# Block maxima over TensorE instead of a DRAM trip, a new load order in the setup, and a second key buffer

## The chip, the cores and the metric

The kernel runs on one core of one Trainium2 chip. The metric is the device time of one execution in microseconds (us); the figure that counts is the median of several executions.

## The reference, cut to what matters

One decoding step of a hybrid block for a prompt of 2048 tokens and 64 sample tokens (NT = 2112 columns) that share the weights:

```python
ada = silu(c) @ w_ada + b_ada            # shift, scale, gate
h = rmsnorm(x) * (1 + scale) + shift
proj = h @ w_in                          # 1024 x 11272, all projections at once
o_att = dilated attention of 8 heads over 3 groups, dilation 1, 4, 16, window 128,
        group outputs weighed by their softmax denominators
a = (o_att * silu(z_a)) @ w_pa
m = mLSTM branch, chunkwise recurrence @ w_pm
y = x + gate * ((sigmoid(g_a) * a + sigmoid(g_m) * m) @ w_out)
```

All of it is float32, and the kernel reaches that accuracy with fp16 matmuls: each 1024 x 128 block of weights is divided by a power of two near its largest magnitude and split into a high and a low fp16 half, and a product is three matmuls (high by high, low by high, high by low).

## The kernel before, in words

The program runs in stages. The **setup** loads `w_ada` in eight pieces (`wa_load`, L439; `ada_cols`, L474), normalises x, builds the halves `hh` and `hl` of h, and splits the first Q, K and V blocks (`first`). The **attention** takes 12 units in a row, 4 head pairs by 3 groups (`units`). While unit i computes scores, softmax and values (`attn`), the projections of unit i+1 (`fill`), the statistics, mixing and weighing of the pair just finished (`late`, L1334) and the splitting of the weights of the unit after that (`prepare`, L1045) are woven in. Then come the mLSTM **recurrence**, the **gates** stage (`all_gates`, L2237, the gate projections in tiles j = 1 to 7, woven with the attention of the sample tokens, `all_samples`, which reads the caches in `kt` and `vt` tiles; after them the steps `f_step` that load, measure and split the last weights), and the **output** stage.

What sets the order: `weave` (L615) runs several generators by their stated costs, and TensorE executes in just that order (its instructions are stamped). VectorE (DVE), ScalarE (ACT), GpSimd (POOL) and SyncE (SP, which issues most loads) execute each in the order the scheduler gave them; `behind()` (L226) keeps an operation behind the last one traced on DVE and ACT.

The way of a weight block, in class `Blocks`: `measure_pieces` reduces each block along its rows on DVE (L257) into a column of `mx`; then the maximum over the 128 partitions is needed in all partitions. Before the change there are two ways for it. One is a trip through DRAM on POOL's queue: `max_begin` writes the columns to `md` (L209) and reads them back broadcast to all partitions into `mb` (L212), and `max_end` reduces that on DVE (L217). The other, used in the setup and for the last weights, is TensorE: `pow2_begin` transposes the columns, padded to 128 x 128 (`zpad`, L183), DVE reduces the rows (L186), and `pow2_end` broadcasts the result with a small matmul (L191) that DVE reads (L193). Either way DVE then makes the scale `wsc`, ACT writes the high half (L281), DVE the low half (L282), and from the same maximum DVE makes `iqk` (L919 to L923), which the scores of the next unit need.

```python
 def max_begin(mx, n, mb=None):
     md = dr.tile([4, P], F32, tag="md", bufs=4, name="md")
     nc.gpsimd.dma_start(dview(md, 0, [[1, P], [P, n]]), mx)
...
     nc.gpsimd.dma_start(mb[:, :n], dview(md, 0, [[0, P], [P, n], [1, P]]))
```

Other names: `pr` is a tile of scores (DVE L1096, then ACT's exponential L1099, then its transpose on TensorE L1107 into `pTs`, then the values L1121); `ktok` (one buffer) holds keys turned to tokens, which SP writes out; `wb` the group weights that `weigh` (L1245) multiplies onto `og`; `whl` the split halves, `wr` a raw block; `ps_mm`, `ps_t`, `ps_s`, `ps_o` are PSUM banks.

Of the kernel before, what the change touches and what calls it, by code (L numbers as in the profile page):

```python
# [19 lines left out]
P = 128  # L20
# [17 lines left out]
ZM = 16  # L38
# [66 lines left out]
def trunk(ctx: ExitStack, tc: tile.TileContext, I, C, O, dbg=None, stop=None):  # L105
# [25 lines left out]
    def pst():  # L131
        return bank("t")
# [34 lines left out]
    zrow = [const.tile([P, 1], F32, name=f"zrow{k}") for k in range(4)]  # L167
    for t in zrow:
        nc.gpsimd.memset(t, 0.0)

    def max_room(pool):
        zpad[:] = [pool.tile([P, P], F32, name=f"zpad{k}") for k in range(1)]
        for t in zpad:
            nc.gpsimd.memset(t, 0.0)

    def max_cols():

        zpad.append(zpad.pop(0))
        return zpad[-1]

    def pow2_begin(mx, n):
        pt = pst()
        nc.tensor.transpose(pt[:, :P], mx, ident)  # L183
        zrow.append(zrow.pop(0))
        m1 = zrow[-1]
# [17 lines left out]
    def max_all(mx, n, mb=None):  # L203

        return max_end(max_begin(mx, n, mb), n)

    def max_begin(mx, n, mb=None):
        md = dr.tile([4, P], F32, tag="md", bufs=4, name="md")
        nc.gpsimd.dma_start(dview(md, 0, [[1, P], [P, n]]), mx)  # L209
        if mb is None:  # L210
            mb = small.tile([P, 2, P], F32, tag="mb", bufs=2, name="mb")
# [24 lines left out]
    class Blocks:  # L236
# [16 lines left out]
        def measure_pieces(self, way=None):  # L253
            n = self.n
            mx = max_cols() if way else small.tile([P, n], F32, tag="mx", name="mx")
            for i, (r, nk, nw) in enumerate(self.raws):
                nc.vector.tensor_reduce(mx[:, i:i + 1], r[:, :nk, :nw], axis=AX.XY, op=OP.max, apply_absolute_value=True)  # L257
                if i + 1 < n:
                    yield
            if way:  # L260
                self.p2, self.mb = way(mx, n), None
            else:
                self.mb = max_begin(mx, n, cur["mb"]() if n > 2 else None)
# [28 lines left out]
        def measure(self, way=None):  # L292
            for _ in self.measure_pieces(way):
                pass
# [71 lines left out]
    with sbuf("setup", side="right") as su:  # L366
# [78 lines left out]
        max_room(su)  # L445
# [9 lines left out]
        first = Blocks([w_in[:, o:o + P] for o in (QO, KO, VO)], inv_sh, WFLOOR)  # L455
# [24 lines left out]

        rows = su.tile([56, P], F32, name="rows")
        nc.sync.dma_start(rows[0:32], I["conv_w"][0].rearrange("j (a p) -> (j a) p", p=P))
        for k, nm_ in enumerate(("conv_b", "m_norm", "m_skip")):
            nc.sync.dma_start(rows[32 + 8 * k:40 + 8 * k], I[nm_][0].rearrange("(a p) -> a p", p=P))
        pt = pss()
        nc.tensor.transpose(pt[:, :56], rows, ident[:56, :56])
        chp = su.tile([P, 56], F32, name="chp")
        nc.vector.tensor_copy(chp, pt[:, :56])
        sc = su.tile([96, 2, P], F32, name="sc")
        nc.sync.dma_start(sc, I["state_conv"][0].rearrange("b j (k p) -> (b j k) p", p=P).rearrange("(a r) p -> r a p", a=2))  # L490
        pt = pss()
        for a in range(2):
            nc.tensor.transpose(pt[:, a * 96:(a + 1) * 96], sc[:, a], ident[:96, :96])
        scT = su.tile([P, 8, 24], F32, name="scT")
        nc.vector.tensor_copy(scT, pt[:, :192].rearrange("p (r k) -> p k r", k=8))

        rt = su.tile([32, 24], F32, name="rt")
        nc.sync.dma_start(rt, I["rel_table"])
        oh = su.tile([32, 3, BANDL], F32, tag="oh", name="oh")
        nc.sync.dma_start(oh, C["onehot"])  # L500
# [1937 lines left out]
```

## Time and profile before

| what | value |
|---|---|
| median of 3 executions | 3099.41 us (3095.2 to 3103.61) |
| the profiled execution, its own time | 3101.56 us |
| its span | 3099.8 us |
| TensorE (PE) busy | 2919.9 us, 94% |
| DVE, ACT, POOL busy | 1534.0, 895.7, 355.2 us |
| mean granted TensorE clock | 0.978 of full |
| DMA, mean over the span | 116 GB/s |

Busy time tells which engine carries the kernel; where it stands idle, and for whom, is in the waits. In a row of the timeline the first number is the start in us, the second the duration, and the bracket at the end holds the time that the engine stood idle just before, and who ended it. PEclk is the clock that TensorE was granted, 1.00 for 2.4 GHz and 0.50 for 1.2 GHz. An engine that is off the path may wait for nothing.

### The profile page before, as it was taken

How to read it: one execution, taken by the hardware profiler on the slowest of the kernel's cores; microseconds unless marked ns; L12 is line 12 of the kernel's file. 1: busy time of each engine (PE TensorE's matmuls, PEld its weight loads, DVE VectorE, ACT ScalarE, POOL GpSimd, SP SyncE). 2: the span in 40 equal slices, each digit the busy share in tenths (PEclk: the TensorE clock that was granted, in tenths of full speed). 3: DMA queues.
4: the chain of work that ended last, by engine and by line, in shares of the span. 5: the costliest groups of instructions: out<-in, count | busy, mean ns of one | idle time of the engine just before them, and what ended most of it. 6: DMA issues, size and time to landing. Idle time of an engine off the chain costs nothing. (4 is left out here: it accounts for less than half of the span.)

```text
span 3099.8 us, 49229 instructions
## 1 busy us (share of the span) xinstructions
PE 2919.9 (94%) x19725; PEld 1573.5 (51%) x19725; DVE 1534.0 (49%) x3832; ACT 895.7 (29%) x2002; POOL 355.2 (11%) x500
## 2 busy tenths in 40 slices
PE   6799999999999999999999999999799989999998
PEld 3455554555555545545455555555465544544443
DVE  4544445444544354475676766755322235445443
ACT  3333332333243224422232222322222223222211
POOL 0100021001101010111111111100100011011011
PEclk9899999999999999999999999999899999999999
DMA  9023332232223232153556433213777753433321
GB/s 326 19 87 96 110 85 69 88 111 83 72 88 108 87 107 55 34 141 102 157 126 204 103 96 92 64 44 76 232 235 222 212 151 123 135 124 115 103 89 61
DMA packets 272825, 358.87 MB, mean 116 GB/s; under 512 B 35348, under 2 KB 204324, under 8 KB 270548
## 3 DMA queue, kind: packets, MB, share of 16 engines
q1 hardware_dynamic: 258500, 242.89, 27.2%
q0 software_dynamic: 14096, 112.83, 11.6%
q8 instruction: 155, 2.54, 0.4%
q14 instruction: 74, 0.61, 0.1%
HBM read 292.99 MB, written 150.04 MB: 143 GB/s over the span
## 5 line engine op out<-in xcount | busy, mean ns | idle before, releaser
L587 PE MATMUL ps_mm<-hh,whl 128*128 128x512 f16 (+1 forms) x3072 | 1022.6, 350 | 17.8 <-ACT whl L281 4.8
L588 PE MATMUL ps_mm<-hl,whl 128*128 128x512 f16 (+1 forms) x3072 | 1022.9, 349 | 0.0
L589 PE MATMUL ps_mm<-hh,whl 128*128 128x512 f16 (+1 forms) x3072 | 1018.4, 349 | 2.2 <-DVE whl L282 2.2
L589 PEld LDWEIGHTS <-whl 128*128 128x128 f16 x3104 | 301.3, 99 | 311.7 <-issue 12.1
L587 PEld LDWEIGHTS <-whl 128*128 128x128 f16 x3104 | 303.9, 99 | 267.1 <-issue 48.8
L588 PEld LDWEIGHTS <-whl 128*128 128x128 f16 x3104 | 301.2, 99 | 243.7 <-issue 21.3
L1099 ACT ACTIVATE pr<-pr,nm 128x256 f32<-128x256 f32 (+1 forms) x384 | 172.7, 450 | 248.0 <-DVE nm L1096 247.6
L1096 DVE CUSTOM_DVE_ANT_0 pr<-ps_s,bias,iqk 128x256 f32<-128x256 f32 (+1 forms) x384 | 141.2, 420 | 92.9 <-PE ps_s L1090 92.9
L1107 PE MATMUL ps_t<-ident,pr 128*128 128x128 f32 x600 | 105.7, 282 | 36.2 <-ACT pr L1099 25.1
L281 ACT ACTIVATE whl<-wr,wsc 128x1024 f16<-128x1024 f32 x80 | 89.0, 1140 | 128.4 <-DVE wsc L200 116.2
L1107 PEld LDWEIGHTS ps_t<-ident,pr 128*128 128x128 f32 x600 | 76.5, 143 | 82.2 <-ACT pr L1099 44.0
L282 DVE SCALAR_TENSOR_TENSOR whl<-wr,wsc,whl 128x1024 f16<-128x1024 f32 x80 | 100.6, 1281 | 35.3 <-ACT whl L281 34.9
L2379 DVE SCALAR_TENSOR_TENSOR tgl<-tgl,ps_mm 128x512 f32<-128x512 f32 x64 | 44.0, 687 | 131.0 <-PE ps_mm L589 131.0
L157 DVE COPY pTs<-ps_t 128x512 f32<-128x512 f32 (+1 forms) x93 | 52.2, 562 | 114.0 <-PE ps_t L1107 113.9
L589 PE MATMUL ps_o<-wouh,gtl 128*128 128x512 f16 (+1 forms) x272 | 103.1, 379 | 0.2 <-DVE gtl L2401 0.2
L587 PE MATMUL ps_o<-wouh,gth 128*128 128x512 f16 (+1 forms) x272 | 103.1, 379 | 0.2 <-DVE y L2346 0.2
L588 PE MATMUL ps_o<-woul,gth 128*128 128x512 f16 (+1 forms) x272 | 103.1, 379 | 0.0
L1121 PE MATMUL ps_o<-pTs,v 128*64 128x128 f32 x1200 | 89.6, 284 | 10.1 <-DVE pTs L157 9.7
L152 ACT ACTIVATE pTs<-ps_t 128x512 f32<-128x512 f32 (+1 forms) x99 | 50.3, 508 | 164.3 <-PE ps_t L1107 164.3
L588 PE MATMUL ps_mm<-mlo,wpmh 128*128 128x512 f16 x256 | 97.0, 379 | 0.0
L587 PE MATMUL ps_mm<-mhi,wpmh 128*128 128x512 f16 x256 | 97.0, 379 | 0.0
L589 PE MATMUL ps_mm<-mhi,wpml 128*128 128x512 f16 x256 | 97.0, 379 | 0.0
(538 smaller groups left out, 4146.2 us busy)
## 6 DMA issues: line engine op xcount, KB each, us to landing
out_dram<-in_cache_kv_w_dram POOLq DMA_DIRECT2D x32, 2040.0 KB, 9.6
wr<-in_w_in_dram SPq DMA_DIRECT2D x80, 512.0 KB
kt<-in_cache_kv_w_dram SPq DMA_DIRECT2D x104, 256.0 KB
vt<-in_cache_kv_w_dram SPq DMA_DIRECT2D x104, 256.0 KB
tgl<-tg_d SPq DMA_DIRECT2D x64, 256.0 KB
out_dram<-in_cache_kv_w_dram POOLq DMA_DIRECT2D x8, 2016.0 KB, 14.8
tg_d<-tg POOLq DMA_DIRECT2D x56, 256.0 KB, 3.9
xt<-in_x_prompt_dram SPq DMA_DIRECT2D x24, 512.0 KB
```

The source lines that it names most:

```text
L152: nc.scalar.activation(out, in_, AF.Copy)
L157: nc.vector.tensor_copy(out, in_)
L281: nc.scalar.activation(hv, rv, AF.Copy, scale=s[:, i:i + 1])
L282: nc.vector.scalar_tensor_tensor(lv, rv, s[:, i:i + 1], hv, op0=OP.mult, op1=OP.subtract)
L587: nc.tensor.matmul(out, lhsT=ah, rhs=bh, start=first, stop=False)
L588: nc.tensor.matmul(out, lhsT=ah, rhs=bl, start=False, stop=False)
L589: nc.tensor.matmul(out, lhsT=al, rhs=bh, start=False, stop=last)
L1096: nc.vector.tensor_tensor_reduce(pr[ti][:, h, :nk], pS[h][:, a:b], bias[:, h, W - nk:W], scale=iqk[:, 2:3], scalar=3.0e38, op0=OP.add, op1 ...
L1099: nc.scalar.activation(pr[ti][:, h, :nk], pr[ti][:, h, :nk], AF.Exp, scale=-1.0, bias=nm[:, h, ti:ti + 1], accum_out=sm[:, h, ti:ti + 1])
L1107: nc.tensor.transpose(pT[:, (h * nb + b2) * P:(h * nb + b2 + 1) * P], pr[ti][:, h, b2 * P:(b2 + 1) * P], ident)
L1121: nc.tensor.matmul(po[h * 64:h * 64 + 64, jc:jc + P], lhsT=x["v"][(k0 + b2) // 4][:, (k0 + b2) % 4, h * 64:h * 64 + 64], rhs=pTs[ti][:, h ...
L2379: nc.vector.scalar_tensor_tensor(tg[:, :n], tg[:, :n], 1.0, pb[:, :n], op0=OP.add, op1=OP.mult)
```

## The change

- The TensorE way becomes the rule in `Blocks`; only the recurrence keeps the DRAM trip (`measure(True)`). Its first half is a step of its own, `turn()` (transpose and row reduce), and its second half (the broadcast) stands at the split. 21 of 32 trips are replaced: 42 DMAs fewer on POOL's queue, 21 transposes and 21 broadcast matmuls more on PE. `turn()` is placed a step ahead of the split in `prepare`, `last_mix`, `z_last` and `all_gates`.
- `zpad` becomes four pads, in a pool that stays; the broadcast of the last weights goes to another PSUM bank (`room=pss`).
- The setup loads all eight `wa` pieces right behind the first quarter of x, then the first weight blocks; the small tables (`rows`, `sc`, `rel_table`, `onehot`, `band`) and what is computed of them move behind the loads of the other quarters of x. The first split stands behind all of `ada_cols`.
- `ktok` gets a second buffer.
- `late` mixes first, then does the next unit's projections and turns, and weighs last, each step of it with 1.25 times its cost.
- In the gates stage the measuring of block pair 2 moves from the end of the recurrence to the gate tile j = 1, the splits of pairs 2 and 3 move back by some steps, and the next load as well.

```diff
-    def pow2_end(m1, n, floor=2.0 ** -100):
-        pb = pst()
+    def pow2_end(m1, n, floor=2.0 ** -100, room=pst):
+        pb = room()
...
-        def measure_pieces(self, way=None):
+        def measure_pieces(self, dram=False):
             n = self.n
-            mx = max_cols() if way else small.tile([P, n], F32, tag="mx", name="mx")
+            self.mx = small.tile([P, n], F32, tag="mx", name="mx") if dram else max_cols()
...
+        def turn(self):
+            self.m1 = pow2_begin(self.mx, self.n)
...
-            p2 = self.p2 if self.mb is None else max_end(self.mb, n)
-            to_pow2(p2, self.floor)
+            if self.mb is not None:
+                p2 = max_end(self.mb, n)
+                to_pow2(p2, self.floor)
+            else:
+                if self.m1 is None:
+                    self.turn()
+                p2 = pow2_end(self.m1, n, self.floor)
...
         for q in range(NWA):
             ada_cols(q)
-
-        rows = su.tile([56, P], F32, name="rows")
...
+            wa_load(NWA + q)
+        first = Blocks([w_in[:, o:o + P] for o in (QO, KO, VO)], inv_sh, WFLOOR)
         with behind():
             x_norm(x0)
-        first.measure(pow2_of)
+        for q in range(NWA, 8):
+            ada_cols(q)
+        first.measure()
         first.split(later=True)
-        for q in range(NWA, 8):
-            wa_load(q)
-            ada_cols(q)
...
-                kt = at.tile([P, 4, P], F32, tag="ktok", bufs=1, name="ktok")
+                kt = at.tile([P, 4, P], F32, tag="ktok", bufs=2, name="ktok")
...
             if step:
+                with behind():
+                    ahead.turn()
+                yield
                 yield from queued(ahead.split_pieces())
...
             if units[i][1] == 2:
-                yield from combine(i)
+                begin_combine(i)
+                yield from tail[3]()
             yield 1
...
+            if units[i][1] == 2:
+                for cost in tail[4]():
+                    yield 1.25 * cost
...
-    def f_split(i):
...
-        p2 = pow2_end(m1, 1)
+        p2 = pow2_end(m1, 1, room=pss)
...
                     if j == 1 and at == 0:
                         with behind():
+                            pend[2].measure()
+                    if j == 1 and at == 1:
+                        with behind():
+                            pend[2].turn()
+                    if j == 1 and at == 3:
+                        with behind():
                             pend[2].split()
                             pend[3].measure()
+                    if j < 6 and at == GS[0] - 2 + 5 * (j == 1):
+                        with behind():
+                            pend[j + 2].turn()
...
-                    if j < 6 and at == GS[0]:
+                    if j < 6 and at == GS[0] + 4 * (j == 1):
                         with behind():
                             pend[j + 2].split()
```

How the rows of the engines move, at three places. First DVE, in the attention, at the split of the four blocks of unit 5 (at 555 us in the trace of before); before:

```order
L159 TENSOR_SCALAR vT<-ps_mm,wun 128x4x128
L257 TENSOR_REDUCE mx<-wr 128x1
L157 COPY pTs<-ps_t 128x512
L217 TENSOR_REDUCE p_5224<-mb_5197 128x4
L221 TENSOR_SCALAR p_5224<-p_5224 128x4
L222 TENSOR_SCALAR p_5224<-p_5224 128x4
L199 RECIPROCAL wsc<-p_5224 128x4
L267 TENSOR_SCALAR wun<-p_5224,inv_sh 128x4
L200 TENSOR_SCALAR wsc<-wsc 128x4
L919 TENSOR_SCALAR iqk<-wun,qk_e 128x2
```

After the change, the same place up to the row reduce:

```order
L269 TENSOR_REDUCE zpad<-wr 128x1
L1293 TENSOR_REDUCE amax<-zall 128x1
L159 TENSOR_SCALAR vT<-ps_mm,wun 128x4x128
L269 TENSOR_REDUCE zpad<-wr 128x1
L157 COPY pTs<-ps_t 128x512
L198 TENSOR_REDUCE zrow_70<-ps_t 4x1
L1123 ISA pr,nm<-ps_s,bias,iqk 128x256
```

and, after four pairs of score rows (L1123, was L1096), the split itself:

```order
L157 COPY og<-ps_o 128x16x32
L954 SCALAR_TENSOR_TENSOR QS<-ps_mm,qk_e,QS 128x4x128
L208 TENSOR_SCALAR p_5302<-ps_t 128x4
L209 TENSOR_SCALAR p_5302<-p_5302 128x4
L214 RECIPROCAL wsc<-p_5302 128x4
L281 TENSOR_SCALAR wun<-p_5302,inv_sh 128x4
L215 TENSOR_SCALAR wsc<-wsc 128x4
L937 TENSOR_SCALAR iqk<-wun,qk_e 128x2
L944 TENSOR_SCALAR uq<-wun 128x1
```

The reduce of the DRAM trip's tile (L217) is gone. In its place the short row reduce (L198) follows the last block's maximum, scores come between, and the scale begins with L208, which reads the broadcast of TensorE.

Second SP, the loads of the setup; before:

```order
L441 DMA wa<-in_w_ada_dram 128x8x256 x4
L412 DMA xt<-in_x_prompt_dram 128x1024 x4
L250 DMA wr<-in_w_in_dram 128x8x128 x3
L482 DMA rows<-in_conv_w_dram 32x128
L484 DMA rows<-in_conv_b_dram 8x128
L484 DMA rows<-in_m_norm_dram 8x128
L484 DMA rows<-in_m_skip_dram 8x128
L490 DMA sc<-in_state_conv_dram 96x2x128
L498 DMA rt<-in_rel_table_dram 32x24
L500 DMA oh<-in_const_onehot_dram 32x1152
L502 DMA bm<-in_const_band_dram 128x384
L441 DMA wa<-in_w_ada_dram 128x8x256 x4
```

After:

```order
L461 DMA wa<-in_w_ada_dram 128x8x256 x4
L432 DMA xt<-in_x_prompt_dram 128x1024 x4
L461 DMA wa<-in_w_ada_dram 128x8x256 x4
L261 DMA wr<-in_w_in_dram 128x8x128 x3
L261 DMA wifr<-in_w_in_dram 128x8x8
L540 DMA xsm<-in_x_sample_dram 64x1024
L432 DMA xp<-in_x_prompt_dram 128x1024 x8
L432 DMA xt<-in_x_prompt_dram 128x1024 x4
L544 DMA rows<-in_conv_w_dram 32x128
L546 DMA rows<-in_conv_b_dram 8x128
L546 DMA rows<-in_m_norm_dram 8x128
L546 DMA rows<-in_m_skip_dram 8x128
```

The second four pieces of `wa` come ahead of the weight blocks (`wr`) and of the small tables, which now follow all of x.

Third the start of the gates stage on DVE; before:

```order
L2041 COPY qm_20565<-qs 64x4x4x2
L2043 COPY qm_20569<-qs 64x4x8
L217 TENSOR_REDUCE p_20690<-mb 128x2
L221 TENSOR_SCALAR p_20690<-p_20690 128x2
L222 TENSOR_SCALAR p_20690<-p_20690 128x2
L199 RECIPROCAL wsc<-p_20690 128x2
L267 TENSOR_SCALAR wun<-p_20690,inv_sh 128x2
L200 TENSOR_SCALAR wsc<-wsc 128x2
L282 SCALAR_TENSOR_TENSOR whl<-wr,wsc,whl 128x1024 x2
L2250 TENSOR_REDUCE amax<-a_20574 128x1
L840 TENSOR_SCALAR u2g<-wun 128x1
L157 COPY kTs<-ps_t 128x512 x2
```

After:

```order
L2071 COPY qm_20544<-qs 64x4x4x2
L2073 COPY qm_20548<-qs 64x4x8
L2288 TENSOR_REDUCE amax<-a_20553 128x1
L208 TENSOR_SCALAR p_20682<-ps_t 128x2
L209 TENSOR_SCALAR p_20682<-p_20682 128x2
L214 RECIPROCAL wsc<-p_20682 128x2
L281 TENSOR_SCALAR wun<-p_20682,inv_sh 128x2
L215 TENSOR_SCALAR wsc<-wsc 128x2
L859 TENSOR_SCALAR u2g<-wun 128x1 x2
L302 SCALAR_TENSOR_TENSOR whl<-wr,wsc,whl 128x1024 x2
L157 COPY kTs<-ps_t 128x512 x2
```

and on SP, before and then after:

```order
L1999 DMA ks<-ks_d 128x12x64
L2247 DMA a_20574<-a_d 128x2048
L2030 DMA kt<-in_cache_kv_w_dram 128x512 x6
L250 DMA wr<-in_w_in_dram 128x8x128 x2
L2030 DMA vt<-in_cache_kv_w_dram 128x512 x3
```

```order
L2029 DMA ks<-ks_d 128x12x64
L2285 DMA a_20553<-a_d 128x2048
L2060 DMA kt<-in_cache_kv_w_dram 128x512 x6
L2060 DMA vt<-in_cache_kv_w_dram 128x512 x7
L2060 DMA kt<-in_cache_kv_w_dram 128x512 x2
```

On DVE the split at this place begins with a TensorE broadcast (L208) and stands behind the reduce of `amax`; on SP the weight loads that stood between the first six `kt` and the first `vt` loads are gone from there.

## Rows read from the trace of the kernel before

**Rows 1.** Waits of PE: what stood idle for whom: us in total, times, longest us.

```profile
PE ps_t L1107 <- ACT pr L1099: 25.1, 15, 4.4
...
PE ps_o L2115 <- DMA vt<-in_cache_kv_w_dram: 10.0, 12, 2.1
PE ps_o L1121 <- DVE pTs L157: 9.7, 4, 3.1
PE ps_t L183 <- DVE p L193: 7.6, 7, 2.4
...
PE ps_t L1107 <- DVE iqk L920: 6.4, 1, 6.4
```

**Rows 2.** Timeline, start of gates: start us, us, instruction, [idle before <-releaser].

```profile
2196.26 0.21 PE L587 MATMUL ps_mm<-hh,whl 128*128 128x64 f16 x1 [3.83 <-ACT tg L844]
...
2207.74 0.42 DVE L217 TENSOR_REDUCE p<-mb 128x2 f32<-128x256 f32 x1 [8.97 <-DMA mb<-md]
...
2211.54 1.57 SPq L250 DMA_DIRECT2D wr<-in_w_in_dram  x2
...
2215.62 1.12 PE L2061 MATMUL ps_t<-ident,kt 128*128 128x128 f32 x4 [12.27 <-DVE kTs L157]
```

**Rows 3.** Waits of DVE, columns as in rows 1.

```profile
DVE p L217 <- DMA mb<-md: 72.1, 14, 10.5
...
DVE ktok L159 <- DMA out_dram<-ktok: 20.3, 3, 7.3
```

**Rows 4.** Timeline of the split of unit 5, columns as in rows 2.

```profile
542.14 0.80 POOL L209 DMA_DIRECT2D md<-mx  x1 [5.14 <-DVE mx L257]
551.81 0.54 POOL L212 DMA_DIRECT2D mb<-md  x1 [8.87 <-DMA md<-mx]
...
555.42 0.69 DVE L217 TENSOR_REDUCE p<-mb 128x4 f32<-128x512 f32 x1 [10.17 <-DMA mb<-md]
...
560.59 1.18 PE L1107 MATMUL ps_t<-ident,pr 128*128 128x128 f32 x4 [4.02 <-ACT pr L1099]
```

**Rows 5.** Windows: length, busy us (instructions) of five engines, PEclk, DMA share, GB/s.

```profile
251.00:258.00 7.00, 6.49 (x26) 3.42 (x28) 3.11 (x10) 1.39 (x3) 0.81 (x2) 0.56 1.00 355
560.00:565.00 5.00, 4.36 (x14) 2.02 (x15) 3.27 (x9) 4.10 (x11) 0.00 (x0) 0.66 1.12 406
...
367.00:374.00 7.00, 6.96 (x32) 3.68 (x33) 3.07 (x10) 3.33 (x10) 0.00 (x0) 0.55 0.89 246
670.00:674.00 4.00, 4.00 (x23) 2.24 (x24) 2.71 (x9) 2.41 (x9) 0.00 (x0) 0.57 1.04 268
968.00:974.00 6.00, 5.91 (x26) 3.06 (x27) 2.85 (x10) 2.65 (x9) 0.00 (x0) 0.50 1.00 275
...
2206.00:2220.00 14.00, 4.38 (x35) 3.04 (x35) 7.55 (x15) 4.05 (x6) 1.07 (x2) 0.51 0.63 193
```

**Rows 6.** Timeline of the setup: SP's second `wa` loads, DVE's first split, PE's first projection.

```profile
28.78 7.91 SPq L441 DMA_DIRECT2D wa<-in_w_ada_dram  x4
...
44.83 3.67 DVE L282 SCALAR_TENSOR_TENSOR whl<-wr,wsc,whl 128x1024 f16<-128x1024 f32 x3
...
59.33 1.01 PE L587 MATMUL ps_mm<-hh,whl 128*128 128x512 f16 x2 [1.76 <-DVE hh L434]
```

**Rows 7.** Window of the first 50 us, columns as in rows 5.

```profile
0.00:50.00 50.00, 27.87 (x174) 16.49 (x178) 19.15 (x47) 9.57 (x14) 1.79 (x14) 0.99 0.95 293
```

**Rows 8.** Timeline of PE at the split of unit 2.

```profile
251.51 1.08 PE L1107 MATMUL ps_t<-ident,pr 128*128 128x128 f32 x4 [6.41 <-DVE iqk L920]
```

**Rows 9.** Timeline of PE where a broadcast and a transpose stand between projections.

```profile
2574.32 0.28 PE L191 MATMUL ps_t<-ident,zrow 128*128 128x1 f32 x2
2574.46 0.31 PE L183 MATMUL ps_t<-ident,zpad 128*128 128x128 f32 x1
2574.60 0.38 PE L587 MATMUL ps_mm<-hh,whl 128*128 128x512 f16 x1
```

**Rows 10.** Window of the gates stage behind its start, columns as in rows 5.

```profile
2220.00:2400.00 180.00, 175.67 (x2005) 109.29 (x1998) 52.48 (x142) 42.09 (x70) 14.92 (x27) 0.99 0.76 242
```

More of the change, by code (lines that the diff above doesn't have):

```diff
@@ L166, in trunk, with max_room @@
     zpad = []
-    zrow = [const.tile([P, 1], F32, name=f"zrow{k}") for k in range(4)]
-    for t in zrow:
+    zrow = [[const.tile([P, 1], F32, name=f"zrow{k}"), False] for k in range(4)]
+    for t, _ in zrow:
         nc.gpsimd.memset(t, 0.0)
-    def max_room(pool):
-        zpad[:] = [pool.tile([P, P], F32, name=f"zpad{k}") for k in range(1)]
-        for t in zpad:
+    def max_room():
+        zpad[:] = []
+        for k in range(2):
+            t = small.tile([P, 2, P], F32, tag="mb", bufs=2, name="zpad")
             nc.gpsimd.memset(t, 0.0)
+            zpad.extend([t[:, j], False] for j in range(2))
+    max_room()
     def max_cols():
         zpad.append(zpad.pop(0))
-        return zpad[-1]
+        assert not zpad[-1][1]
+        zpad[-1][1] = True
+        return zpad[-1][0]
     def pow2_begin(mx, n):
@@ L201, in up_scale, with max_begin @@
         return s
-    def max_all(mx, n, mb=None):
-        return max_end(max_begin(mx, n, mb), n)
-    def max_begin(mx, n, mb=None):
+    def max_begin(mx, n):
         md = dr.tile([4, P], F32, tag="md", bufs=4, name="md")
         nc.gpsimd.dma_start(dview(md, 0, [[1, P], [P, n]]), mx)
-        if mb is None:
-            mb = small.tile([P, 2, P], F32, tag="mb", bufs=2, name="mb")
+        mb = small.tile([P, 2, P], F32, tag="mb", bufs=2, name="mb")
         nc.gpsimd.dma_start(mb[:, :n], dview(md, 0, [[0, P], [P, n], [1, P]]))
@@ L557, in trunk @@
         xc = [x0] + [x_load(c) for c in (1, 2, 3)]
+        rows = su.tile([56, P], F32, name="rows")
+        nc.sync.dma_start(rows[0:32], I["conv_w"][0].rearrange("j (a p) -> (j a) p", p=P))
+        for k, nm_ in enumerate(("conv_b", "m_norm", "m_skip")):
+            nc.sync.dma_start(rows[32 + 8 * k:40 + 8 * k], I[nm_][0].rearrange("(a p) -> a p", p=P))
+        pt = pss()
+        nc.tensor.transpose(pt[:, :56], rows, ident[:56, :56])
+        chp = su.tile([P, 56], F32, name="chp")
+        nc.vector.tensor_copy(chp, pt[:, :56])
+        sc = su.tile([96, 2, P], F32, name="sc")
+        nc.sync.dma_start(sc, I["state_conv"][0].rearrange("b j (k p) -> (b j k) p", p=P).rearrange("(a r) p -> r a p", a=2))
+        pt = pss()
+        for a in range(2):
+            nc.tensor.transpose(pt[:, a * 96:(a + 1) * 96], sc[:, a], ident[:96, :96])
+        scT = su.tile([P, 8, 24], F32, name="scT")
+        nc.vector.tensor_copy(scT, pt[:, :192].rearrange("p (r k) -> p k r", k=8))
+        rt = su.tile([32, 24], F32, name="rt")
+        nc.sync.dma_start(rt, I["rel_table"])
+        oh = su.tile([32, 3, BANDL], F32, tag="oh", name="oh")
+        nc.sync.dma_start(oh, C["onehot"])
+        bm = su.tile([P, BANDL], F32, tag="bm", name="bm")
+        nc.sync.dma_start(bm, C["band"][0:1].to_broadcast([P, BANDL]))
+        eb = su.tile([P, 3, BANDL], F32, tag="eb", name="eb")
+        rt16 = su.tile([32, 24, 16], F32, name="rt16")
+        nc.vector.tensor_copy(rt16, rt[:, :, None].to_broadcast([32, 24, 16]))
+        for g in range(3):
+            pb = pst()
+            nc.tensor.matmul(pb[:, :BANDL], lhsT=rt16[:, 8 * g:8 * g + 8].rearrange("b h r -> b (h r)"), rhs=oh[:, g, :],
+                             start=True, stop=True)
+            nc.vector.tensor_add(eb[:, g], pb[:, :BANDL], bm)
+        keep("chp", P, [56], chp)
+        keep("scT", P, [8, 24], scT)
+        band_out(0, 0, 32)
         for g, p0 in ((0, 32), (1, 0), (2, 0)):
@@ L1353, in last_mix @@
                         early["o"].measure()
+            with behind():
+                early["o"].turn()
             tail[1]()
@@ L1375, in z_last @@
                         early["z"].measure()
+                if k == ZM + 14:
+                    with behind():
+                        early["z"].turn()
         weights[0] = first
@@ L1969, in trunk @@
         return
+    max_room()
     phg = ExitStack()
```

90 lines of the change are left out of this document (32 added, 58 removed).

## The prediction, made before the run

> **What bounds the kernel.** I read three views. The busy shares first: TensorE works 94% of the span, so the end is set by its stream, and only what shortens that stream or its idle time counts. Then the waits of PE [rows 1]: read which instruction stood, and for whom. The largest (L1107 for `pr` 25.1 us, for `iqk` 6.4; L1121 for `pTs` 9.7) and one of 12.27 for `kTs` [rows 2] name ACT and DVE, which are half idle. So the third view is what those engines waited for [rows 3]: DVE stood 72.1 us for the DRAM trip of the maxima, 20.3 us for the writing out of `ktok`. The chain is plain at one split [rows 4]: POOL issues the write at 542.14, the read only at 551.81, DVE gets the tile at 555.42 after 10.17 us of standing, and all that is queued behind it on DVE, scores of the running unit among it, is late, so PE stands 4.02 us at 560.59. Last the windows [rows 5]: behind each such stall PE is granted 1.2 GHz for some us; the loss is the window's length times one less PEclk. All this is against the profiled execution, 3101.56 us, 2.15 above the median of the three runs.
>
> **A, setup.** In before the second four `wa` pieces are issued at 28.78 and the first projection starts at 59.33 [rows 6]. DMA is 95% busy at 293 GB/s until 50 [rows 7]; by the tiles' sizes eight `wa` of 1.05 MB, four `xt` and three `wr` of 0.52 MB must land before it, 12.1 MB, 41 us at that rate. The change puts them in one row. Behind the last `wr` stand its maximum, the turn, the scale, three low halves (3.67 us [rows 6]) and the first `hh`, some 11 us by estimate: 52 to 54, so 5 to 7 us earlier. The small tables' copies and sums on DVE, an estimated 2 to 3 us of short work, move behind that projection, where DVE makes the halves `hh` and `hl` that PE waits for, and give part of it back. Their loads now queue behind 12 x tiles on SP; the bias that comes of them is first needed by unit 0's scores, behind all projections of the setup, which cover that. Bounds: 8 gained (the whole earlier start), 1 lost (start no earlier, part of the small work late). I take **−4**.
>
> **B, maxima in the attention.** Of the waits for `pr` and `iqk`, 31.5 us [rows 1], seven stand at a split: 6.41 and 4.02 [rows 4, 8], and of the same form two of 4.39 and three of 1.3 to 1.6, in all 23.5 us. The clock behind them costs 7 × 0.44 = 3.1 at the first, 5 × 0.34 = 1.7 at the one at 560 [rows 5]; with the two others of that kind at 1.7 each, 8.2. Gross 31.7 us. After the change DVE's order has the row reduce where the transpose is just done, then scores, then the scale, and PE has some 9 us of projections between transpose and broadcast: nothing waits for a DMA. The split itself still comes between scores (DVE alone 3.67 us for three blocks [rows 6]), so a part of the waits stays: bounds 10 and 32, I take **−27**, near the upper end, since the row names the DMA for 10.17 us and PE stands for less than half of that.
>
> The row is the argument here: from write to read 9.67 us, to the tile 13.3 us [rows 4]. The Trainium skill, page "DMA: Bandwidth & Descriptors", section "Anatomy of one DMA — SWDGE (gpsimd) path", gives a transfer about 2.0 us of fixed cost. By that the trip would take about 4 us as an estimate, DVE, which came to it at 545.25, would have stood under 1 us, and B would be worth next to nothing. The trace disagrees, with 13.3 us at this place.
>
> **C, second `ktok`.** DVE waits 3 times, 20.3 us in all, for the keys to leave [rows 3]; PE stands behind it in three of the four waits of L1121, 7.7 of 9.7 us [rows 1]. The clock costs 7 × 0.45 + 4 × 0.43 + 6 × 0.50 = 7.9 [rows 5]. With two buffers the waiting copy finds a free one; the third copy in a row can still meet the first one's write. Bounds 4 and 15.6, I take **−12**.
>
> **D, weighing last and paced.** About 8 us of PE's waits, the rest of L1107 and the fourth of L1121 [rows 1], stand where `weigh` packs DVE. In the new order it still stands closely before the reduce of `amax`, only later. Bounds +6 (it now collides with the next unit's scores) and −8; I take **−2**, near no change, since DVE's instructions are the same.
>
> **E, start of the gates.** PE stands 3.83 us for a `tg` behind a split, then 12.27 us for `kTs` copies that lie behind the second split, whose trip DVE awaits 8.97 us [rows 2]; the window behind it loses 4.4 × 0.49 = 2.1 [rows 5]. Gross 18.2. SP, too, holds the first `vt` loads behind a `wr` that only the split frees, at 2211.54 [rows 2]; in the new order they follow the first `kt` at once. Bounds 0 (see the third rival) and 18; I take **−15**.
>
> **Costs.** A broadcast and a transpose between projections take 2574.60 − 2574.32 = 0.28 us [rows 9]; 21 of each, **+6**. Each can also wait for DVE and hold all projections behind it: 7 transposes did so in before, 1.1 us each, 2.4 at most [rows 1]. The bounds over 42 are 0 and 46; I take **+4**, since the new ones stand a step apart from what feeds them. The broadcast of the last weights in another bank may spare some of those 7.6 us, or nothing, since the transposes behind it also need the next block; I take 0, bounds −7.6 and 0. POOL's 42 DMAs, two more memsets and the shorter reduces lie on engines that have slack: 0.
>
> **Sum:** −4 −27 −12 −2 −15 +6 +4 = −50, so 3101.6 − 50 = 3051.6, and 3049 as a median.
>
> **Rivals.**
> 1. *Half comes back.* PE runs its stream in order; a transpose whose maximum is late stops projections that did not wait before, and DVE's scale now waits for PE. For it: the 7 waits [rows 1]. Against: the 9 us between the two steps. Half of the 60 gained: 3049 + 30 = 3079. The Trainium skill, page "TensorE: Matmul & The Clock Gate", section "Step-by-step: what each phase is for", says that matmuls stay in program order and only weight loads are pulled ahead; by that a late maximum stops everything behind it, and the time would be this 3079 rather than my sum. The waits of L183 [rows 1] agree with the rule.
> 2. *Slower.* The same waits, at every insertion, at PE's two ends of the turn: 42 at the 1.1 us seen, and behind one in four a stretch at 1.2 GHz that costs 2.5 (the mean loss of the first five windows [rows 5]), 42 × 1.7 = 71 in place of my 4. That gives 3049 + 67 = 3116. It decides from 1.3 us each on. Against: 22 of the 29 transposes of before waited for no such read.
> 3. *The gates stage is held by DMA.* Behind its start the engines move 242 GB/s at a share of 0.76 [rows 10], and PE waits 10.0 us for `vt` [rows 1]. Then the 15 of E return as such waits: 3064.
> 4. *All of it.* The gross of A to E, 8 + 31.7 + 15.6 + 8 + 18.2 = 81.5, less 6: 3099.4 − 75.5 = 3024.
> 5. *It does not do what it says:* the stalls' true holder is the splitting itself (three or four blocks on ACT and DVE between scores), not the trip. Then only C and a little of E are left, less the costs: within 9 us of before.
>
> **Chances.** Forecast 0.42; rival 1 0.22, rival 2 0.05, rival 3 0.14, rival 4 0.12, rival 5 0.05. A measurement of this kernel tells apart about 0.3%, 9.3 us. Faster by over that: 0.90; within: 0.05; slower by over that: 0.05. The range of 8 in 10 leaves out rivals 2 and 5 and the outer half of rival 4: 3022 to 3084.
>
> **What would show it.** In the profile after: no wait of DVE for `mb` in the attention; PE's waits of L1107 for `pr` and `iqk` down from 31.5 to under 8; no wait of `ktok` for its writing; PE's idle time near 2196 and 2215 under 4 us together; first projection at 52 to 54. PE waiting for the new transposes or broadcasts by over 15 us together would be rival 1; over 60, rival 2; waits for `vt` of over 20, rival 3. I am wrong if PE's idle time falls as told but its stream grows, or if the waits at the splits stay with another releaser.

## The result and the profile after

| | before | after |
|---|---|---|
| median of 4 executions each, same chip | 3101.51 us (3095.2 to 3106.28) | 3031.66 us (3027.26 to 3036.04) |
| span of the profiled execution | 3099.8 us | 3025.5 us |
| PE busy | 2919.9 us | 2887.7 us |
| mean granted TensorE clock | 0.978 | 0.988 |

The ratio is 0.9778, interval 0.9762 to 0.9793: 70 us faster, where 50 were forecast. The profiled spans differ by 74.3 us, and the account below is made of these two. The lines moved: L183 is now L190, L191 is L206, L1107 is L1134, L1121 is L1148, L2061 is L2091, L2115 is L2145.

The waits of PE after the change, to be held against [rows 1]:

```profile
PE ps_t L190 <- DVE zpad L269: 20.9, 3, 16.0
PE ps_o L1148 <- ACT pr L1126: 10.5, 1, 10.5
PE ps_t L190 <- DVE p L208: 8.4, 7, 1.6
...
PE ps_t L1134 <- DVE pTs L157: 2.8, 3, 0.9
PE ps_t L1134 <- ACT pr L1126: 2.6, 6, 0.6
...
PE ps_t L2091 <- DVE kTs L157: 1.0, 1, 1.0
...
PE ps_t L206 <- DVE zrow L198: 0.7, 2, 0.4
```

At the transposes L1107, now L1134, scores that came late cost 31.5 us in before and 2.6 now; the 12.27 us for `kTs` are 1.0; the waits for `vt`, 10.0 us, are gone altogether, and nobody had counted on that. Two large waits are new, each at a single place: 10.5 us at the product L1148, whose releaser is a late score `pr` as well, and 16.0 at a transpose L190.

Where along the program the time was won is read from instructions that both traces have. In before, PE's first idle row of the gate rows, the end of the attention, the recurrence's first transposes, its last ones, and the first transpose of the output stage:

```profile
228.57 0.21 PE L720 MATMUL ps_t<-ident,gat 64*1 64x64 f32 x1 [1.96 <-DVE gat L713]
...
1300.19 0.71 PE L1107 MATMUL ps_t<-ident,pr 128*128 128x128 f32 x2 [0.58 <-ACT pr L1099]
...
1448.31 1.30 PE L1657 MATMUL ps_t<-ident,hr 128*128 128x128 f32 x4 [0.47 <-DVE hr L1716]
...
2170.10 0.66 PE L1657 MATMUL ps_t<-ident,hr 128*128 128x128 f32 x4 [2.51 <-DVE zo L1646]
...
2507.87 0.30 PE L183 MATMUL ps_t<-ident,zpad 128*128 128x128 f32 x1 [1.92 <-DVE zpad L2156]
```

The same five after the change, the first projection ahead of them, and the two new stalls and the start of the gates between them:

```profile
51.77 1.01 PE L606 MATMUL ps_mm<-hh,whl 128*128 128x512 f16 x2 [4.70 <-DVE hh L454]
...
222.44 0.21 PE L739 MATMUL ps_t<-ident,gat 64*1 64x64 f32 x1 [1.96 <-DVE gat L732]
...
518.87 1.98 PE L1148 MATMUL ps_o<-pTs,v 128*64 128x128 f32 x16 [10.47 <-ACT pr L1126]
...
1253.82 0.71 PE L1134 MATMUL ps_t<-ident,pr 128*128 128x128 f32 x2 [0.57 <-ACT pr L1126]
...
1305.32 0.47 PE L190 MATMUL ps_t<-ident,zpad 128*128 128x128 f32 x1 [16.00 <-DVE zpad L269]
...
1409.11 1.30 PE L1688 MATMUL ps_t<-ident,hr 128*128 128x128 f32 x4 [0.47 <-DVE hr L1747]
...
2131.19 1.11 PE L1688 MATMUL ps_t<-ident,hr 128*128 128x128 f32 x4 [2.72 <-DVE zo L1677]
...
2161.82 0.66 PE L2091 MATMUL ps_t<-ident,kt 128*128 128x128 f32 x4 [1.00 <-DVE kTs L157]
...
2438.63 0.33 PE L190 MATMUL ps_t<-ident,zpad 128*128 128x128 f32 x1 [1.66 <-DVE zpad L2184]
```

Subtract row by row. The setup won 6.1 us; the attention 40.2 (the lead grows from 6.1 to 46.4); the passage into the recurrence gave back 7.2 (to 39.2); the recurrence, whose code stayed, changed by 0.3; the gates stage won 30.3 (to 69.2); what follows 5.1, to 74.3. In windows between these rows, 42.1 of the 74.3 us are idle time of PE and 32.2 its busy time, though it executes 63 matmuls more: in the attention 24.9 and 15.3, in the gates stage 24.4 and 6.0. The busy time fell as more of the stream ran at the higher clock: the mean clock of the gates stage was 0.96 and is 0.99. In a window of 6 us behind the stall at 518.87 PE was granted 0.55, that is near 1.2 GHz, while in the gates stage behind its start [rows 10] the clock is 1.00 now:

```profile
518.00:524.00 6.00, 5.13 (x25) 2.84 (x26) 2.50 (x5) 1.18 (x3) 5.92 (x5) 0.55 0.01 3
1288.00:1306.00 18.00, 2.00 (x9) 0.75 (x7) 12.77 (x25) 0.10 (x1) 4.09 (x5) 0.60 0.65 187
2220.00:2400.00 180.00, 180.00 (x2127) 113.86 (x2120) 52.27 (x133) 44.22 (x72) 12.94 (x24) 1.00 0.78 250
```

Both new stalls have DVE behind them, as its timeline shows (columns as in rows 2):

```profile
500.75 1.09 DVE L1272 TENSOR_TENSOR wb<-wb,og 128x256 f32<-128x256 f32 x3 [3.53 <-DMA wb<-wt_d]
...
512.70 0.48 DVE L1123 CUSTOM_DVE_ANT_0 pr<-ps_s,bias,iqk 128x256 f32<-128x256 f32 x1
...
1292.59 1.10 DVE L1272 TENSOR_TENSOR wb<-wb,og 128x256 f32<-128x256 f32 x3 [6.55 <-DMA wb<-wt_d]
...
1302.93 2.34 DVE L269 TENSOR_REDUCE zpad<-wr 128x1 f32<-128x1024 f32 x2
```

At the first, DVE waits for the group weights `wb` until 500.75 and then works off a packed run of weighing steps; the scores, ready since the matmuls at 507.57, are touched only at 512.70. At the second, the maxima of the last `o` weights stand behind the weighing that had waited 6.55 us for `wb`. In before their turn came later, at the split; the change put it into PE's stream right there, so PE stood with it.

### The profile page after: what moved, and what is told of

Read it like the earlier page. It is cut to its first block, busy times and chain, and to the rows that moved or that the text cites. A ratio compares the mean times of both kernels' runs of the same rounds, so it can differ in the third digit from the quotient of the medians.

```text
span 3025.5 us, 49245 instructions
## 1 busy us (share of the span) xinstructions
PE 2887.7 (95%) x19788; PEld 1565.6 (52%) x19788; DVE 1526.5 (50%) x3828; ACT 897.5 (30%) x2002; POOL 330.3 (11%) x460
## 5 line engine op out<-in xcount | busy, mean ns | idle before, releaser
L607 PEld LDWEIGHTS <-whl 128*128 128x128 f16 x3104 | 299.9, 98 | 234.6 <-issue 13.1
L1123 DVE CUSTOM_DVE_ANT_0 pr<-ps_s,bias,iqk 128x256 f32<-128x256 f32 (+1 forms) x384 | 141.3, 420 | 104.9 <-PE ps_s L1117 104.6
L157 DVE COPY pTs<-ps_t 128x256 f32<-128x256 f32 (+1 forms) x96 | 54.3, 566 | 131.1 <-PE ps_t L1134 131.0
L1134 PE MATMUL ps_t<-ident,pr 128*128 128x128 f32 x600 | 101.9, 277 | 7.1 <-DVE pTs L157 2.8
L1134 PEld LDWEIGHTS ps_t<-ident,pr 128*128 128x128 f32 x600 | 76.1, 141 | 47.7 <-ACT pr L1126 13.8
L1148 PE MATMUL ps_o<-pTs,v 128*64 128x128 f32 x1200 | 88.4, 283 | 12.5 <-ACT pr L1126 10.5
L863 ACT ACTIVATE tg<-ps_mm,u2g 128x512 f32<-128x512 f32 (+1 forms) x74 | 45.3, 614 | 181.2 <-PE ps_mm L608 168.2
L152 ACT ACTIVATE pTs<-ps_t 128x256 f32<-128x256 f32 (+1 forms) x96 | 48.5, 506 | 164.9 <-PE ps_t L1134 164.9
```

The costliest lines, as they stand in the source:

```text
L152: nc.scalar.activation(out, in_, AF.Copy)
L157: nc.vector.tensor_copy(out, in_)
L607: nc.tensor.matmul(out, lhsT=ah, rhs=bl, start=False, stop=False)
L863: nc.scalar.activation(tg[:, :n], pg, AF.Tanh, scale=u2)
L1123: nc.vector.tensor_tensor_reduce(pr[ti][:, h, :nk], pS[h][:, a:b], bias[:, h, W - nk:W], scale=iqk[:, 2:3], scalar=3.0e38, op0=OP.add, op1 ...
L1134: nc.tensor.transpose(pT[:, (h * nb + b2) * P:(h * nb + b2 + 1) * P], pr[ti][:, h, b2 * P:(b2 + 1) * P], ident)
```

## The experiments

All were made later than the first comparison and, by the times, on other chips: the kernel before took 3128.6 to 3132.5 us there, about 1% longer, and the changed kernel 3037.2, 0.2% longer. So each run is held against the changed kernel there, whose span in the profile is 3039.2. A ratio is to the kernel before, run beside it. All share one chip but the run of the unused trip, which was on a second one, with the kernel before at 3130.2.

**The control.** The changed kernel, unaltered.

> The changed kernel itself once more, beside the three runs that follow, so that each is compared with it on the same chip. Theory and rival alike: the ratio to before that was measured, 0.976 to 0.980 on a like chip; on a chip where loads are slower, as in the last runs, a ratio of 0.970 to 0.975, since the gates stage of before waits for loads that the change brings earlier.

Measured: 3037.23 us (3035.62 to 3040.97), ratio 0.9716, 0.9696 to 0.9736. Differences of medians below are to this, unless said otherwise. The ratio's interval is 0.2% to either side, some 6 us.

**A, the setup's order undone.**

```diff
+        first = Blocks([w_in[:, o:o + P] for o in (QO, KO, VO)], inv_sh, WFLOOR)
...
-            wa_load(NWA + q)
-        first = Blocks([w_in[:, o:o + P] for o in (QO, KO, VO)], inv_sh, WFLOOR)
+
+        rows = su.tile([56, P], F32, name="rows")
...
-        for q in range(NWA, 8):
-            ada_cols(q)
         first.measure()
         first.split(later=True)
+        for q in range(NWA, 8):
+            wa_load(q)
+            ada_cols(q)
```

The loads and sums of the small tables stand ahead of the first split again.

> The changed kernel with the setup in the order of before (tables and weight blocks first, then the second four wa pieces). Theory: the 7.4 us by which the first turn of V comes earlier in the trace after the change are the worth of the load order, and nothing behind takes them back: 5 to 8 us above the changed kernel, first projection near 59 again. Rival: the pads and the turns behind the split give the start, not the order of the loads: within 3 us.

Measured: 3043.27 us (3037.34 to 3046.45), ratio 0.9731, 0.9709 to 0.9754: 6.0 longer by the medians, though the intervals overlap, with the first projection at 58.21 us. The start moves by some 6 us, and by the medians nothing gives it back; with intervals that overlap this is the likely size, not a sure one.

**C, one buffer for `ktok`.**

```diff
-("ktok", [P, 4, P], F32, 2)
+("ktok", [P, 4, P], F32, 1)
-                kt = at.tile([P, 4, P], F32, tag="ktok", bufs=2, name="ktok")
+                kt = at.tile([P, 4, P], F32, tag="ktok", bufs=1, name="ktok")
```

> The changed kernel with one buffer for the turned keys instead of two, all else as it is. Theory: three waits of DVE of about 7 us for the writing out come back, PE stands behind them 2 to 3 us each and runs at 1.2 GHz for some us after each: 10 to 15 us, 3042 to 3047. Rival: in the new order other work of PE covers the copies: under 3 us, 3030 to 3035.

Measured: 3060.14 us (3054.86 to 3062.61), ratio 0.9779, 0.9764 to 0.9793: 22.9 longer, about twice my term. Its timeline of PE has three stalls; behind the first, the matmuls of 512 columns show as 0.63 us instead of 0.38:

```profile
361.50 1.11 PE L1134 MATMUL ps_t<-ident,pr 128*128 128x128 f32 x4 [3.56 <-ACT ktok L154]
362.40 0.63 PE L606 MATMUL ps_mm<-hh,whl 128*128 128x512 f16 x1
...
364.96 0.38 PE L606 MATMUL ps_mm<-hh,whl 128*128 128x512 f16 x1
...
664.03 0.66 PE L1134 MATMUL ps_t<-ident,pr 128*128 128x128 f32 x4 [3.63 <-ACT ktok L154]
...
956.34 1.11 PE L1134 MATMUL ps_t<-ident,pr 128*128 128x128 f32 x4 [4.30 <-ACT ktok L154]
```

11.5 us of idle time, against 7.7 in the three of before [rows 1]. ACT makes the waiting copy here, where DVE made it in before [rows 3]. The mean clock is 0.981 against the control's 0.984, on 3060 us some 9 us of PE's time at most. Together these two make up most of the difference.

**B, the trip back for the blocks of the attention's units**, on top of one `ktok` (the space of the second is needed for the old tile of four maxima). The four early block pairs `g`, `x`, `o` and `z` stay on TensorE.

```diff
-                with behind():
-                    ahead.turn()
-                yield
                 yield from queued(ahead.split_pieces())
...
-                yield from queued(ahead.measure_pieces())
+                yield from queued(ahead.measure_pieces(True))
```

> As the run with one key buffer, and the maxima of the 11 units' weight blocks taken by the trip through DRAM again; the setup, the early blocks and the gates stay on TensorE. Theory: against the run with one key buffer the waits of DVE for the tile from DRAM return in the attention, some 48 us in ten, and with them 20 to 30 us of PE's time (my B): 3064 to 3075. Rival: the new order of the late work alone keeps the splits clear of the trip: within 6 us of the run with one key buffer, 3042 to 3053.

Measured: 3096.25 us (3092.4 to 3098.97), ratio 0.9897, 0.9881 to 0.9914: 36.1 longer than with one `ktok` alone. The stalls at the splits are there again, with DVE's wait for the trip (its waits, then PE's timeline):

```profile
DVE p L228 <- DMA mb<-md: 62.8, 11, 11.7
```

```profile
245.00 1.09 PE L1132 MATMUL ps_t<-ident,pr 128*128 128x128 f32 x4 [7.89 <-DVE iqk L939]
...
559.45 1.18 PE L1132 MATMUL ps_t<-ident,pr 128*128 128x128 f32 x4 [5.01 <-ACT pr L1124]
...
861.68 1.18 PE L1132 MATMUL ps_t<-ident,pr 128*128 128x128 f32 x4 [5.56 <-ACT pr L1124]
...
1169.16 1.18 PE L1132 MATMUL ps_t<-ident,pr 128*128 128x128 f32 x4 [5.56 <-ACT pr L1124]
```

So the trip, not the splitting itself, held the scores: this kernel splits the same blocks and differs in where the maxima come from. The stall near 519, still there with one `ktok` alone (10.8 us), is absent here: it came with the maxima on TensorE and the order on DVE that goes with them, so the 36.1 us are what is left after it.

**D, weighing in the old place, without the factor 1.25.**

```diff
                 yield from tail[3]()
+                yield from tail[4]()
...
-            if units[i][1] == 2:
-                for cost in tail[4]():
-                    yield 1.25 * cost
```

> The changed kernel, with the order of the late work as before: mixing and weighing first, then the next unit's projections, without the factor 1.25. Theory: weighing last is worth little by itself (my D, 2 us), and its one large wait, 10.47 us of PE at 518.87 plus some 3 us of clock, goes; the old small waits of 1.6 to 2.7 us at three pairs return, some 7 us: 3024 to 3032. Rival: weighing last is what keeps DVE free at the splits, and with the old order the waits at the splits return though no DRAM trip is there, 3 times 4 us and clock: 3040 to 3050.

Measured: 3040.69 us (3038.44 to 3044.73), ratio 0.972, 0.9706 to 0.9735: no difference from the control. Around the first stall the weighing, the scores and the maxima stand in the same order on DVE as with the change (elsewhere a maximum moves by a step), and both new stalls are there, with 10.70 and 15.53 us. The edit did not move what it meant to move, so the run does not test whether weighing last would help.

**E, the trip back for the gates' blocks.** The pads are then made at the output stage, since the trip's tile needs their place.

```diff
-                            pend[j + 3].measure()
+                            pend[j + 3].measure(True)
...
-                            pend[j + 2].turn()
```

> The changed kernel with the maxima of the gates stage by the DRAM trip, at the same places in the program and with the same order of SP's loads. Theory one: with the loads in the new order the waits for vt stay away, and only the start of the stage pays for the trip: 5 to 12 us above the changed kernel, a wait of DVE for the tile from DRAM of 5 to 9 us at the first two splits. Theory two: the trip at the first splits is what costs: 15 to 22 us above, with PE's wait for kTs of about 12 us back.

Measured: 3067.11 us (3065.68 to 3071.85), ratio 0.9808, 0.9785 to 0.9832: 29.9 longer, twice my term. PE waits 14.4 us for `kt` and 10.8 for `vt`:

```profile
2179.91 1.12 PE L2090 MATMUL ps_t<-ident,kt 128*128 128x128 f32 x4 [14.11 <-DMA kt<-in_cache_kv_w_dram]
...
2240.42 0.42 PE L2144 MATMUL ps_o<-vt,pm 128*32 128x128 f32 x8 [2.78 <-DMA vt<-in_cache_kv_w_dram]
```

These are waits for cache loads, not for the maxima. SP issues seven `vt` directly behind the first six `kt` here as well, so the order of SP's loads, to which the prediction gave a part, does not free `vt` by itself. The window of the stall, and then the control's window with the same loads, show the DMA engines busier and yet moving less:

```profile
2165.00:2180.00 15.00, 0.89 (x5) 0.28 (x4) 4.22 (x25) 2.39 (x3) 2.14 (x4) 0.66 1.23 205
```

```profile
2155.00:2165.00 10.00, 9.99 (x69) 4.86 (x67) 4.82 (x24) 1.37 (x2) 1.08 (x2) 1.00 1.06 344
```

**The load of a later block pair back in its old step.**

```diff
-                    if j < 5 and at == GS[1] + (j == 1):
+                    if j < 5 and at == GS[1]:
```

> The changed kernel with the load of pair 4 in the gates stage one step earlier, where it was before the change (on SP it now stands between vt and kt loads). Theory one (the order of SP's loads made a good part of the gates stage's 30 us): the vt and kt loads behind it come late, waits of PE for vt of some 5 to 10 us return, plus clock: 6 to 15 us above the changed kernel. Theory two (the maxima on TensorE made it): the place of one load is worth nothing, within 3 us.

Measured: 3035.63 us (3031.12 to 3041.43), ratio 0.971, 0.9687 to 0.9733: no difference, and no wait for `vt`. Whatever this edit is worth is below what these runs tell apart.

**The trip beside the new way, for nobody.** This parts the two readings of E: someone is late because the maxima are, or the trip itself is in the way. The maxima of the gates go over PE as changed; the same two DMAs are issued as well, and what they bring is not read (they end in DRAM, there being no room for the tile).

```diff
+        def ghost(self):
+            self.measure()
+            n = self.n
+            md = dr.tile([4, P], F32, tag="mdx", bufs=2, name="mdx")
+            nc.gpsimd.dma_start(dview(md, 0, [[1, P], [P, n]]), self.mx[:, :n])
+            mb = dr.tile([P, 2, P], F32, tag="mbx", bufs=2, name="mbx")
+            nc.gpsimd.dma_start(mb[:, :n], dview(md, 0, [[0, P], [P, n], [1, P]]))
```

> The changed kernel, whose maxima of the gates' weights still go over PE, with the DRAM trip issued beside them from POOL at the same places (write of 1 KB in 4-byte packets, read of it as 128 KB), 6 times; nothing reads what the trip brings. With the trip in earnest the gates stage cost 30 us more (3067 against 3037). Theory A, those 30 us are latency: whoever waits for the maxima comes late, and with nobody waiting the time stays within 5 us of the changed kernel on the same chip (3037, ratio 0.9716), with waits of PE for cache loads below 5 us in all. Theory B, the trip's small packets and POOL's standing for them hold up the cache loads themselves: 12 us or more slower, PE waits for kt near the start of the gates and for vt behind it of 10 us or more together. In between (5 to 12 us): both have a part, read from the waits for kt and vt.

Measured: 3069.43 us (3064.22 to 3077.18), ratio 0.9811, 0.9791 to 0.9832. Theory B: by the ratio, the trip that nobody awaits costs what the trip in earnest costs. Its waits of PE, then of its timeline SP's queue, POOL's, and PE's longest wait for `vt`:

```profile
PE ps_o L2153 <- DMA vt<-in_cache_kv_w_dram: 11.6, 7, 6.5
...
PE ps_t L2099 <- DMA kt<-in_cache_kv_w_dram: 5.4, 2, 3.7
```

```profile
2152.15 0.59 SPq L2025 DMA_DIRECT2D sbl<-sb_d  x1
2156.88 0.59 SPq L2025 DMA_DIRECT2D sbias<-sb_d  x1
...
2167.14 0.72 POOL L320 DMA_DIRECT2D mdx<-zpad  x1 [9.13 <-DVE zpad L269]
2178.94 0.55 POOL L322 DMA_DIRECT2D mbx<-mdx  x1 [11.07 <-DMA mdx<-zpad]
2179.48 1.62 POOL L872 DMA_DIRECT2D tg_d<-tg  x3
...
2458.35 0.65 PE L2153 MATMUL ps_o<-vt,pm 128*32 128x128 f32 x8 [6.48 <-DMA vt<-in_cache_kv_w_dram]
```

POOL stands 11.07 us between write and read, and three writes of gate tiles `tg` leave together behind it. SP has a gap of 4 us among the small loads that stand ahead of `kt`, where the control has none. And the cache loads land late. The control's chip and this one differ, so the stage is compared by its length, from the recurrence's last transposes to the output stage's first: 337.8 us in before, 307.4 after the change, 313.2 in the control, 338.8 with the trip in earnest, 341.9 with the trip for nobody. In the 15 us from the first of the `kt` issues at 2164.7, the DMA engines show 241 GB/s here at a share of 0.99: less moved than in the control, as in the run before, but at no higher share. Which share the small packets have and which POOL's standing was not separated.

The trace of before agrees. Its 12 waits for `vt` all come within 18 us behind one of the last four of the stage's six writes of maxima by POOL, at 2256.32, 2330.52, 2406.22 and 2477.01. Two of the four, each with the longest wait behind it:

```profile
2330.52 0.71 POOL L209 DMA_DIRECT2D md<-mx  x1 [2.06 <-DVE mx L257]
...
2341.45 0.43 PE L2115 MATMUL ps_o<-vt,pm 128*32 128x128 f32 x8 [2.13 <-DMA vt<-in_cache_kv_w_dram]
...
2477.01 0.71 POOL L209 DMA_DIRECT2D md<-mx  x1 [3.03 <-DVE mx L257]
...
2485.48 0.42 PE L2115 MATMUL ps_o<-vt,pm 128*32 128x128 f32 x8 [1.56 <-DMA vt<-in_cache_kv_w_dram]
```

**The turn of the last weights, not early.**

```diff
-            with behind():
-                early["o"].turn()
             tail[1]()
```

> The changed kernel, with the turn of block pair o taken out of the last mixing; it is done where the pair is split, at the start of the recurrence. In the trace after the change PE stands 16.0 us at that turn (1305.32), since the maximum lies on DVE behind the weighing, which waits for its weights from DRAM. Theory: in PE's order the turn came too early and held projections of the recurrence behind it; without it the 16 us and about 2 us at half clock go, and some 8 to 10 us come back at the start of the recurrence, where before the change about 6 us of waits and 4 us of clock stood: 3020 to 3025. Rival: the projections behind the turn need what comes later anyway, so the wait only moves: within 4 us of the changed kernel, 3028 to 3036.

Measured: 3028.94 us (3026.98 to 3033.37), ratio 0.9683, 0.9669 to 0.9698. The stall of 16 us is gone; what takes its place is 2.08 us and three of under 1:

```profile
1332.96 0.39 PE L606 MATMUL ps_o<-hh,whl 128*128 128x512 f16 x1 [2.08 <-ACT whl L301]
1334.00 0.39 PE L606 MATMUL ps_mm<-hh,whl 128*128 128x512 f16 x1 [0.43 <-ACT whl L301]
1335.38 0.39 PE L608 MATMUL ps_o<-hh,whl 128*128 128x512 f16 x1 [0.78 <-DVE whl L302]
```

The median falls by 8.3 us, and the recurrence's first transposes come at 1398.02 instead of 1409.19. By the medians this kernel beats both. It ran again beside the next two:

> The changed kernel without the early turn of the last projection's maxima (the o weights), as in the first run of this study, here as the control beside the two below. Expected: ratio 0.968 to the kernel before again (0.9669 to 0.9698 the first time), the idle of some 16 us at the transpose L190 near 1305 absent, the idle of some 10.8 us near 519 ahead of the product L1148 still there.

Measured: 3029.16 us (3026.75 to 3035.79), ratio 0.968, 0.9662 to 0.9699.

**The stall at 519, two other mixes.** On that kernel, one number of the weave: when a pair's first attention enters it.

```diff
-LAG = 0.3
+LAG = 0.4
```

> The control with one number more changed: the attention of a pair's first unit enters the weave at 0.4 instead of 0.3, so that on DVE the first pair's weighing steps L1272 to L1274 stand behind the scores L1123 more evenly (two runs of weighing ahead of the next pair of scores where there were three with the read of a block between). Theory A, the stall near 519 is DVE's packed weighing alone: the 10.8 us of idle there fall below 4 and with the slow-clocked matmuls behind them (some 1.4 us) the time is 8 to 10 us under the control. Rival B, the steps only move: as much idle comes back at a transpose L1134, L190 or a product L1148 within 60 us, and the time is within 3 us of the control. Rival C, the later attention leaves PE without work or pushes the units' splits late: 5 us or more slower than the control.

Measured: 3044.76 us (3042.38 to 3047.75), ratio 0.9724, 0.9706 to 0.9741: 15.6 longer than its control. The stall moves, to the projection behind the copy of `vT`, which now stands last in the same run of weighing, and to a block's maximum:

```profile
518.59 0.59 PE L606 MATMUL ps_mm<-hh,whl 128*128 128x512 f16 x1 [8.73 <-ACT vT L154]
...
530.38 0.45 PE L190 MATMUL ps_t<-ident,zpad 128*128 128x128 f32 x1 [3.77 <-DVE zpad L269]
```

> The same with 0.5: on DVE the five last weighing steps of the first pair stand in one run behind the scores, followed by the blocks' maxima L269, and the row reductions L198 of unit 3k+2's blocks come after the scores of the next unit. Theory A (packed weighing ahead of scores sets the stall): the idle near 519 falls below 4, but the maxima come later, so that a wait at the transpose L190 or at the split's broadcast L206 of some 2 to 5 us per pair takes its place; 0 to 8 us under the control. Rival B (the steps only move): within 3 us of the control. Rival C: 5 us or more slower than the control, with waits at L606 for the late weights.

Measured with 0.5: 3042.29 us (3038.84 to 3049.81), ratio 0.9719, 0.9698 to 0.9739, 13.1 longer, with 17.9 us of waits for `vT` in three places.

Both are slower by more than a stall that only moved would make them. With 0.4, the waits for `vT` and for a block's maximum at L190 come to 24.1 us, where the control has 15.0 with its stall; which new overlap makes the rest was not followed. By their times both are rival C. A run of weighing steps comes at once on DVE when `wb` lands, some 1.9 us each; whatever PE needs and is queued behind them waits. Why only the first pair is hit with the chosen number stays open.

## Why the prediction was right, and where it was not

The direction, the engine and the chain were right: PE's idle time behind the DRAM trips and the single `ktok` was the loss, and it went. The time came 17 us under the forecast, inside its range; rival 4, all of it at 3024, lies nearer to it than the forecast does, and the range was wide. By its parts, the second column as undone on the other chip:

| part | forecast | measured, us |
|---|---|---|
| A setup | 4 | 6.0; on the first chip 6.1 |
| B maxima in the attention | 27, less some 5 of the 10 for insertions | 36.1 for the 11 units, their insertions and the new stall included |
| C second `ktok` | 12 | 22.9 |
| D weighing last | 2 | 3.5 in a run that did not test it, and not told from nothing |
| E gates | 15 | 29.9; on the first chip 30.3 |

The parts add up to 98, against 91 between the two kernels on that chip and 70 on the first one, so B and C can't be carried over one to one. On the first chip the whole attention won 40.2, with the new stall of 10.5 in it, where B, C, D and half of the insertions made 36.

The sum was short on the clock more than on idle time. B, C and E held 18.2 us of clock at most, less 6 for the new matmuls; PE's busy time fell by 32.2.

- **A** is right by its mechanism: first projection at 51.77, where 52 to 54 were said, and of the 7.6 us by which it starts earlier all but 1.4 are left at the end of the setup.
- **B**: the releaser named was the right one, and rival 5 (the splitting itself) falls with the run that brought the trip back. Two of the signs came as told: no wait of DVE for `mb` in the attention, scores at 2.6 us where under 8 were asked. What B did not have is the 10.5 us at L1148, a fresh packing of DVE: the weighing ahead of the next unit's scores, which D's upper bound named and priced at 6.
- **C** was mis-sized. The term took the idle time and clock of before; in the changed kernel the same single buffer costs 11.5 us idle instead of 7.7. That other stalls covered part of the wait in before is my reading of it and was not tried apart. The sign given, no `ktok` waiting for its writing, came.
- **D**, a step by itself, failed as an edit: DVE's order did not follow. Its "about 8 us" are 10.0 by the rows it names: 8.0 of L1107 and 2.0 of L1121.
- **E** is the step that failed most. The sign given, idle time near 2196 and 2215 under 4 us, came with 1.00, though the control on the later chip has 4.8 there. That DVE's standing for the trip held the copies `kTs` stays as [rows 2] show it. But I left the 10.0 us for `vt` where they were, as a matter of the stage's DMA load. The unused trip, and the places of these waits in before, put them down to the trips: where a trip is under way the cache loads come late, whether or not anyone awaits it. So the waits for `vt` went with the trips, and rival 3 had the sign of it wrong: the stage still moves 250 GB/s at a share of 0.78, and PE waits for no load. The Trainium skill, page "DMA: Bandwidth & Descriptors", section "Anatomy of one DMA — SWDGE (gpsimd) path", says that a transfer's fixed cost is mostly its completion, and can be surprisingly long when the target is HBM. That agrees in kind: the write of 1 KB took 9.7 us to land at the median of the six. The 2.0 us that it gives do not.
- **Costs.** The insertions cost what was said at all places but one: waits at the transposes (L183, now L190) rose from 13.4 to 34.4 us, 16.0 of it at the turn of `o`; the other 5.0 against the 4 set down. Rival 1's mechanism, a late maximum that stops PE's stream, is real and happened there; its sign, over 15 us at the new transposes, came with that one wait, but not its time. With the other PSUM bank for the last weights the waits there are 8.4 us against 7.6 [rows 1], the longest 1.6 instead of 2.4. What follows the gates won 5.1 us that no term had, 3.8 of them in PE's busy time: in before the clock falls to 0.83 behind its longest wait there, 3.41 us, and after the change no wait there is over 1.7. Whether the bank did that was not tried.

## What to carry to other kernels

Price a round trip through DRAM by running it for nobody: here that cost about as much as waiting for it, because other loads came late beside it. When a step is put into the stream of an engine that runs in order, look at what its input is queued behind on the engine that makes it; of all the insertions, the one behind a wait for a DMA cost 16 us, and leaving it out won 8. And an edit to a planner's order counts only once the engine's own order is seen to have changed.

## What the runs showed of the hardware

- A trip of 1 KB out and 128 KB back on POOL's queue, six times in 340 us and read by nobody, made that stretch 341.9 us long, against 313.2 in the control on another chip. In before, all 12 waits for `vt` fall within 18 us behind such a write. With the trip in earnest the DMA engines showed, at the start of the cache loads, a share of 1.23 at 205 GB/s, where they showed 1.06 at 344 without it.
- The later chip took 0.9% longer than the first for the kernel before (3128.6 against 3101.5 us) and 0.2% for the changed one (3037.2 against 3031.7). Of the 13.7 us between the changed kernel's two profiled spans, 5.8 lie in the gates stage. No profile of before was taken on the later chip, so where it loses its 0.9% is open.
